# A hybrid recurrent layer: which engine makes the low parts of the input projection's weights

## The chip, the core and the metric

The kernel runs on one core of a Trainium2 chip. The metric is device microseconds of one execution, as the median of the timed runs; lower is better. The engines are named TensorE (PE in the rows; PEld is its weight load), VectorE (DVE), ScalarE (ACT), GpSimd (POOL) and SyncE (SP, whose queue issues nearly all the DMAs). Each engine works through a queue of its own in order, and waits where an instruction needs the result of another engine.

## What is computed

One layer of a hybrid decoder, for 1024 prompt tokens and 64 sample tokens (8 sequences of 8) together. Only the parts that matter here:

```python
z = jnp.einsum('bld,de->ble', x, p['w_in'])          # 1024 -> 2828 columns
(a_x, a_gate, b_xbc, b_dt, b_gate, c_qkv, c_beta, c_decay, c_gate, d_u, d_gate) = split_cols(z, IN_SPLITS)
ya = rglru_mixer(a_x, ...) * silu(a_gate)            # A: RG-LRU
yb = rms_norm(ssd_mixer(b_xbc, b_dt, ...) * silu(b_gate))   # B: Mamba-2 SSD
yc = gdn_mixer(c_qkv, c_beta, c_decay, ...) * silu(c_gate)  # C: gated delta net
yd = s5_mixer(d_u, ...) * silu(d_gate)               # D: S5
x = layer_norm(ALPHA * x + concat(ya, yb, yc, yd) @ p['w_out'])
```

All of it is float32, with float32 results; the new states of the four mixers are returned too.

## The kernel before

**The products.** TensorE multiplies float32 in three passes: each operand is split into a high part (a copy to the type fp32r) and a low part (the operand less the high part), and the product is high times high, low times high and high times low (L226, L227, L228 for the input projection). `xh` and `xl` hold the input, transposed, 8 tiles of 128 rows by 1088 tokens.

**The channel tiles.** The input projection makes most of its columns as channel tiles, called strips here: 128 channels by 1088 tokens, in three blocks of tokens (320, 384, 384), each a PSUM bank. `gemm_ch` does one strip. It calls `load_w` for the strip's weights, then multiplies block after block; `evac` empties each bank to SBUF, on ScalarE (L242) or, every fourth time, on VectorE (L244). There are 18 strips through `gemm_ch`: six of C_QKV (in the order 2, 3, 0, 1, 4, 5), two of C_AX, four of C_XBC, two gates each for A, D and C. The two strips of C_DU have code of their own (`u_tiles`), and the token-major weights (`gemm_tok`, L398 to L400) call `load_w` with four parts of 128x536.

**The weights.** `load_w` brings a strip's 128x1024 weights in two parts of 128x512. Each part is a DMA into `wr` (two buffers, L151), a copy to the high part `wh` on ScalarE (L156), and a subtraction into the low part `wl` (L157). `wh` and `wl` have four buffers each, which is two strips. So a strip's weights can be made while the strip before is multiplied, and the high part waits until TensorE has left the strip before that. A buffer of `wr` can be loaded again when its low part is made. `lo_eng` is a list that holds VectorE and is never given another engine.

**What is around it.** The S5 mixer runs between the first strips, in two halves. In each half `table` makes a table of powers (L463 to L465 through `cmul`; on VectorE for the first half, on GpSimd for the second), `outs` makes the output weights on GpSimd (L618 to L620), and `half_run` multiplies the table with S5 inputs on VectorE (L463 to L465 again) and scans (L650). `cmul` and `outs` share four temporary buffers. After a C_QKV strip `conv_of` does its convolution (L264 on ScalarE, L266 three times on VectorE) and `keep_tail` copies its last columns on GpSimd (L270, L271). GpSimd also writes the strip's pad columns (L249, L250). From about 200 us on, `gdn` (chunk by chunk, with a matrix inverse in six levels, L846 to L868) is merged with `side`, which holds the other strips, the RG-LRU, the SSD and the output projection. `gdn` uses GpSimd for L801, L824, L839, L901 and L999.

**What sets the order.** The kernel is written with a framework that derives all semaphores, and that also orders each engine's queue itself, from its own estimates of when an instruction can start. The order on an engine is therefore not simply that of the text.

Of the kernel before, what the change touches and what calls it, by code (L numbers as in the profile page):

```python
# [8 lines left out]
F32 = mybir.dt.float32  # L9
# [5 lines left out]
OP = mybir.AluOpType  # L15
# [4 lines left out]
P = 128  # L20
# [22 lines left out]
def seqs(ap):  # L43

    return ap.rearrange("p (b e) -> p b e", e=11)


def toks(ap):
    return ap.rearrange("p (b e) -> p b e", e=8)
# [3 lines left out]
def hybrid_step(ctx, tc, I, O, dbg=None):  # L53
# [4 lines left out]
    V = nc.vector  # L58
    G = nc.gpsimd
# [17 lines left out]
    def nm(s):  # L77
        uid[0] += 1
        return f"{s}_{uid[0]}"
# [9 lines left out]
    def strip(pool, dt=F32, name="s"):  # L89
        return pool.tile([P, SW], dt, name=nm(name), tag="s")  # L90
# [21 lines left out]
    def merge(*streams):  # L112

        live = [[g, 0.0, w] for g, w in streams]
        while live:
            e = min(live, key=lambda e: e[1] / e[2])
            try:
                c = next(e[0])
                e[1] += c
                yield c  # L120
            except StopIteration:
                live.remove(e)
# [14 lines left out]
        c0 = 0 if i == 0 else NS + P * (i - 1)  # L137
        nc.sync.dma_start(x[:n, :1024], I["x"][c0:c0 + n])

    lo_eng = [V]  # L140

    def load_w(src, n, kn=4, pool=None, ready=None):

        his, los = [], []
        if pool is not None:
            kp = 8 if 8 * n <= SW else 4
            big = [[strip(pool, F32R, name=nm_)[:, :kp * n].rearrange("p (k n) -> p k n", k=kp) for _ in range(8 // kp)] for nm_ in ("wh", "wl")]
        for k0 in range(0, 8, kn):
            wr = wp.tile([P, 536], F32, name=nm("wr"), tag="wr", bufs=2)
            wv = wr[:, :kn * n].rearrange("p (k n) -> p k n", k=kn)  # L150
            nc.sync.dma_start(wv, src[:, k0:k0 + kn])  # L151
            if pool is None:
                hv_, lv = (wp.tile([P, 536], F32R, name=nm(t), tag=t)[:, :kn * n].rearrange("p (k n) -> p k n", k=kn) for t in ("wh", "wl"))
            else:
                hv_, lv = (z[k0 // kp][:, k0 % kp:k0 % kp + kn] for z in big)
            act(hv_, wv, AF.Copy)  # L156
            lo_eng[0].tensor_tensor(lv, wv, hv_.bitcast(F32), OP.subtract)  # L157
            his += [hv_[:, k] for k in range(kn)]
            los += [lv[:, k] for k in range(kn)]
        return his, los  # L160

    def w_tile(c0):
        return I["w_tiles"][W_TILES.index(c0)]
# [57 lines left out]
    def gemm_block(w, a, b, evac):  # L221
        whi, wlo = w
        ps = gemm_bank()
        o = ps[:, :b - a]
        for k in range(8):
            mm(o, whi[k], xh[:, k, a:b], start=(k == 0), stop=False)  # L226
            mm(o, whi[k], xl[:, k, a:b], start=False, stop=False)  # L227
            mm(o, wlo[k], xh[:, k, a:b], start=False, stop=(k == 7))  # L228
        evac(a, b, o)

    def gemm_ch(c0, evac):
        w = load_w(w_tile(c0), P)
        for a, b in BLOCKS:
            gemm_block(w, a, b, evac)
            yield 3.7
# [10 lines left out]
    def gemm_strip(c0, key, i, pool):  # L246

        s = strip(pool, name="z")
        G.memset(s[:, 0:3], 0.0)  # L249
        G.tensor_copy(seqs(s[:, 1027:SW])[:, :, 0:3], cached(key, i))  # L250

        def evac(a, b, o):
            if a == 0:
                copy_out(seqs(s[:, 1027:SW])[:, :, 3:11], toks(o[:, :NS]))
                copy_out(s[:, 3:3 + b - NS], o[:, NS:])
            else:
                copy_out(s[:, 3 + a - NS:3 + b - NS], o)

        yield from gemm_ch(c0 + P * i, evac)
        return s  # L260
# [20 lines left out]
    def new_tails():  # L281
        return tmp("tails")[:, :162].rearrange("p (t e) -> p t e", e=27)

    def store_tails(gt, nt, key):
        nc.sync.dma_start(O[key], gt[:, :nt])
# [105 lines left out]
    def gemm_tok():  # L391
        whi, wlo = load_w(I["w_tok"], 268, 2, cs)
        for i in range(9):
            c0 = 0 if i == 0 else NS + P * (i - 1)
            ps = pg.tile([P, 512], F32, name=nm("pg"), tag="g")
            o = ps[:, :268]
            for k in range(8):
                mm(o, xh[:, k, c0:c0 + P], whi[k], start=(k == 0), stop=False)  # L398
                mm(o, xl[:, k, c0:c0 + P], whi[k], start=False, stop=False)  # L399
                mm(o, xh[:, k, c0:c0 + P], wlo[k], start=False, stop=(k == 7))  # L400
            z = strip(cs, name="bg")
            t, g = z[:, :268], z[:, 268:524]
            act(t, o, AF.Copy)
            act(g, t[:, 4:260], AF.Tanh, scale=0.5)
            act(raw[:, i, 0:4], t[:, 0:4], AF.Copy)
            act(raw[:, i, 4:12], t[:, 260:268], AF.Copy)
            stt(g, g, 1.0, t[:, 4:260], OP.add, OP.mult)
            nc.sync.dma_start(bg_d[i], g)
# [885 lines left out]
    def conv_of(s, wkey, bkey, i, nt, tails, silu=True):  # L1294
        acc = conv(s, wkey, bkey, i, nt)
        keep_tail(s, tails[:, i])
        if silu:
            silu_compact(s, acc)
        return s if silu else acc

    def conv_in(c0, key, wkey, bkey, i, nt, pool, tails, silu=True):
        s = yield from gemm_strip(c0, key, i, pool)
        return conv_of(s, wkey, bkey, i, nt, tails, silu)
# [23 lines left out]
    def gate(c0, pool):  # L1327

        g = strip(pool, name="gate")

        def evac(a, b, o):
            act(g[:, a:b], o, AF.Tanh, scale=0.5)
            stt(g[:, a:b], g[:, a:b], 1.0, o, OP.add, OP.mult)

        yield from gemm_ch(c0, evac)
        return g

    def side():
        lo_eng[0] = V
        bw_ = tc.tile_pool(name="bw", bufs=1, reuse_waits="tile")  # L1340
        bw = bw_.__enter__()
        tails, xc, zb = new_tails(), [], []
        for i in range(2):
            xc.append((yield from conv_in(C_AX, "cache_rglru_conv", "rg_conv_w", "rg_conv_b", i, 2, up, tails, silu=False)))
        store_tails(tails, 2, "rg_tails")

        def ahead():
            for i in range(4):
                zb.append((yield from gemm_strip(C_XBC, "cache_ssd_conv", i, up)))

        hA = []
        yield from merge((rglru(bw, up, xc, hA), 20.0), (ahead(), 44.0))
        for i in range(2):
            g = yield from gate(C_AG + P * i, up)
            stt(toks(g[:, :NS]), toks(g[:, :NS]), 0.5, seqs(hA[i][:, NP:CL])[:, :, 3:11], OP.mult, OP.mult)
            stt(g[:, NS:T], g[:, NS:T], 0.5, hA[i][:, :NP], OP.mult, OP.mult)
            mix[i] = g
        tails = new_tails()
        for i in range(4):
            conv_of(zb[i], "ssd_conv_w", "ssd_conv_b", i, 4, tails)  # L1360
            yield 0.0
        store_tails(tails, 4, "ssd_tails")
        yield from merge((ssd(bw, up, zb[0:2], zb[2], zb[3]), 40.0), (gates_cd(), 44.0))
        mix[2:4] = zb[0:2]
        bw_.__exit__(None, None, None)
        yield from project()
# [3 lines left out]
    def gates_cd():  # L1370
        for i in range(2):
            g = yield from gate(C_DG + P * i, up)
            y = strip(cc, name="yD")
            nc.sync.dma_start(y[:, :T], zd_d[i])
            gv = g[:, :T].rearrange("p (c t) -> p c t", t=8)
            stt(gv, gv, 0.25, y[:, :T].rearrange("p (t c) -> p c t", t=8), OP.mult, OP.mult)
            mix[6 + i] = g
        for i in range(2):
            gc[i] = yield from gate(C_CG + P * i, cc)


    def project():
# [18 lines left out]
        for i in range(9):  # L1401
# [44 lines left out]
            else:  # L1446
                for e in (slice(0, 512), slice(512, 1024)):
                    stt(y[:, e], y[:, e], mv[:, 0:1], lnp[0][:, e], OP.subtract, OP.mult)
                for e in (slice(0, 512), slice(512, 1024)):
                    stt(y[:, e], y[:, e], rs, lnp[1][:, e], OP.mult, OP.add)  # L1450
                    nc.sync.dma_start(dst[:, e], y[:, e])

    run(merge((gdn(wk, up, q, k, v, *rn), 130.0), (side(), 280.0)))


# [77 lines left out]
```

## Time and profile before

| | |
|---|---|
| median of 3 runs | 652.92 us (647.18 to 653.27) |
| the profiled execution | 648.38 us, span 646.5 us |
| instructions | 11718 |
| ScalarE busy | 271.6 us, 42% of the span |
| mean granted TensorE clock | 0.976 |

The span goes from the first to the last instruction of the profiled execution; 1.9 us of its time lie around it. The rows below are from this execution. Times in them are in microseconds from the start of the span.

### The profile page before, as it was taken

What the parts mean: (1) busy time and instruction counts of PE and PEld (TensorE: products, weight loads), DVE (VectorE), ACT (ScalarE), POOL (GpSimd) and SP (SyncE); (2) the same over time, 40 slices, a digit from 0 to 9 for tenths busy, and PEclk for the clock granted to TensorE, in tenths of its full rate; (3) what the DMA queues carried; (4) which work ended last, traced back from release to release, by engine and by line L of the source; (5) the groups of instructions that cost most, each with busy time, mean ns of one, the idle gap of its engine ahead of it and who ended that gap; (6) DMA issues with size and microseconds to landing.
All of it is one profiled execution on the core that took longest, in us unless ns stands there. A gap on an engine that the chain in (4) does not pass through costs nothing.

```text
span 646.5 us, 11718 instructions
## 1 busy us (share of the span) xinstructions
PE 589.7 (91%) x4284; PEld 504.0 (78%) x4284; DVE 469.6 (73%) x1378; ACT 271.6 (42%) x677; POOL 180.9 (28%) x305
## 2 busy tenths in 40 slices
PE   3999699499999999988999999999999796999995
PEld 3999699499999786777888877778777564778884
DVE  5996963782559676899897777868777897754443
ACT  5544235143345244854644434354443752333210
POOL 8313119400101322331502032032030122443633
PEclk9999799889899999999999999999999997999998
DMA  8462113032311010100122021001022511013131
GB/s 288 165 191 63 41 34 86 1 96 59 128 57 55 18 36 33 33 18 19 33 69 68 33 89 66 1 17 43 9 75 78 171 43 49 33 55 113 66 117 78
DMA packets 23929, 44.11 MB, mean 68 GB/s; under 512 B 3073, under 2 KB 10193, under 8 KB 23873
## 3 DMA queue, kind: packets, MB, share of 16 engines
q1 hardware_dynamic: 23696, 42.71, 20.1%
q8 instruction: 33, 0.54, 0.4%
q0 software_dynamic: 176, 0.67, 0.3%
q14 instruction: 24, 0.19, 0.1%
HBM read 32.97 MB, written 10.41 MB: 67 GB/s over the span
## 4 chain that ended last, share of the span: by engine, by line
PE 66%; DVE 19%; POOL 5%; issue 5%; ACT 2%; DMA 1%; SPq 0%; DVEq 0%; ACTq 0%; POOLq 0%
PE pg L226 8%; PE pg L227 8%; PE pg L228 8%; PE pg L1428 5%; PE pg L1427 5%; PE pg L1426 5%; DVE tb L846 2%; DVE yb L846 2%; DVE acc L266 2%; PE ssq L755 1%; PE pg L398 1%; DMA x<-in_x_t_dram 1%; PE pg L399 1%; PE pg L400 1%; PE kq L817 1%
## 5 line engine op out<-in xcount | busy, mean ns | idle before, releaser
L226 PE MATMUL pg<-xh,wh 128*128 128x384 f32 (+1 forms) x432 | 150.2, 348 | 9.0 <-DVE z L244 9.0
L227 PE MATMUL pg<-xl,wh 128*128 128x384 f32 (+1 forms) x432 | 149.0, 345 | 0.0
L228 PE MATMUL pg<-xh,wl 128*128 128x384 f32 (+1 forms) x432 | 147.0, 340 | 0.0
L226 PEld LDWEIGHTS pg<-xh,wh 128*128 128x128 f32 x432 | 82.8, 192 | 12.5 <-DVE z L244 9.3
L227 PEld LDWEIGHTS pg<-xl,wh 128*128 128x128 f32 x432 | 82.6, 191 | 2.1 <-issue 0.5
L228 PEld LDWEIGHTS pg<-xh,wl 128*128 128x128 f32 x432 | 82.4, 191 | 1.3 <-issue 0.3
L1426 PE MATMUL pg<-woh,wh 128*128 128x512 f32 (+1 forms) x144 | 58.2, 404 | 1.9 <-ACT wh L1415 1.9
L1427 PE MATMUL pg<-wol,wh 128*128 128x512 f32 (+1 forms) x144 | 58.5, 406 | 0.2
L1428 PE MATMUL pg<-woh,wl 128*128 128x512 f32 (+1 forms) x144 | 57.9, 402 | 0.4 <-DVE wl L1416 0.4
L266 DVE SCALAR_TENSOR_TENSOR acc<-z,pcol,acc 128x1112 f32<-128x1112 f32 x36 | 49.6, 1381 | 5.1 <-ACT acc L264 4.8
L864 ACT ACTIVATE XY<-XY 128x256 f16<-128x256 f32 (+1 forms) x51 | 19.4, 381 | 53.8 <-PE XY L862 48.2
L156 ACT ACTIVATE wh<-wr 128x512 fp32r<-128x512 f32 (+1 forms) x40 | 25.2, 633 | 35.0 <-PE pg L227 28.3
L1429 DVE SCALAR_TENSOR_TENSOR y<-y,pg 128x512 f32<-128x512 f32 (+1 forms) x18 | 12.3, 686 | 32.2 <-PE pg L1428 28.4
L1426 PEld LDWEIGHTS pg<-woh,wh 128*128 128x128 f32 (+1 forms) x144 | 26.6, 184 | 8.9 <-ACT wh L1415 2.2
L1428 PEld LDWEIGHTS pg<-woh,wl 128*128 128x128 f32 (+1 forms) x144 | 26.6, 185 | 7.3 <-DVE wl L1416 0.9
L1427 PEld LDWEIGHTS pg<-wol,wh 128*128 128x128 f32 (+1 forms) x144 | 26.5, 184 | 7.2 <-DVE wol L1393 1.0
L157 DVE TENSOR_TENSOR wl<-wr,wh 128x512 fp32r<-128x512 f32 (+1 forms) x40 | 28.2, 704 | 2.8 <-ACT wh L156 2.4
L857 DVE TENSOR_TENSOR T<-T,lev 128x256 f16<-128x256 f32 (+1 forms) x51 | 21.4, 419 | 10.7 <-PE T L855 10.1
L868 ACT ACTIVATE XY<-XY 128x256 f16<-128x256 f32 (+1 forms) x51 | 19.4, 381 | 22.5 <-PE XY L867 22.5
L242 ACT ACTIVATE z<-pg 128x384 f32<-128x384 f32 (+2 forms) x37 | 14.0, 389 | 34.5 <-PE pg L228 33.2
L846 DVE COPY tb<-T 64x256 f16<-64x256 f16 x99 | 26.2, 264 | 1.6
L846 DVE COPY yb<-XY 64x256 f16<-64x256 f16 x99 | 23.8, 240 | 4.4 <-ACT XY L868 3.0
(453 smaller groups left out, 1398.0 us busy)
## 6 DMA issues: line engine op xcount, KB each, us to landing
wr<-in_w_tiles_dram SPq DMA_DIRECT2D x40, 256.0 KB, 2.9
x<-in_x_t_dram SPq DMA_DIRECT2D x8, 544.0 KB, 6.3
wo<-in_w_out_dram SPq DMA_DIRECT2D x16, 256.0 KB, 2.9
y<-in_x_dram SPq DMA_DIRECT2D x8, 512.0 KB, 3.3
out_y_dram<-y SPq DMA_DIRECT2D x7, 512.0 KB, 2.6
bgd<-bg SPq DMA_DIRECT2D x9, 128.0 KB, 1.8
dud<-us SPq DMA_DIRECT2D x2, 544.0 KB, 4.2
U<-dud SPq DMA_DIRECT2D x16, 68.0 KB, 3.4
```

Of the source, the lines that this page charges most:

```text
L156: act(hv_, wv, AF.Copy)
L157: lo_eng[0].tensor_tensor(lv, wv, hv_.bitcast(F32), OP.subtract)
L226: mm(o, whi[k], xh[:, k, a:b], start=(k == 0), stop=False)
L227: mm(o, whi[k], xl[:, k, a:b], start=False, stop=False)
L228: mm(o, wlo[k], xh[:, k, a:b], start=False, stop=(k == 7))
L266: stt(acc[:, :CL], s[:, j:j + CL], col(wkey, j * nt + i), acc[:, :CL], OP.mult, OP.add)
L846: V.tensor_copy(dst[s, :, s], src[s])
L857: tt(t_[:n], pt[:n], lev[:n, l].unsqueeze(1).to_broadcast([n, 4, 64]), OP.mult)
L864: act(XY[:n, :256], px[:n, :256], AF.Copy)
L1426: mm(ps[:n], mh[k_], woh[:, k_, e], start=(k_ == 0), stop=False)
L1427: mm(ps[:n], mh[k_], wol[:, k_, e], start=False, stop=False)
L1428: mm(ps[:n], ml[k_], woh[:, k_, e], start=False, stop=(k_ == 7))
```

## The change

`load_w` gets an argument `eng` in place of one that was not used, and subtracts on that engine, or on VectorE if none is given. `gemm_ch` gives GpSimd. The list `lo_eng` goes.

```diff
@@ -137,9 +137,8 @@
-    lo_eng = [V]
-
-    def load_w(src, n, kn=4, pool=None, ready=None):
+
+    def load_w(src, n, kn=4, pool=None, eng=None):
@@ -154,7 +153,7 @@
             act(hv_, wv, AF.Copy)
-            lo_eng[0].tensor_tensor(lv, wv, hv_.bitcast(F32), OP.subtract)
+            (eng or V).tensor_tensor(lv, wv, hv_.bitcast(F32), OP.subtract)
@@ -229,7 +228,7 @@
     def gemm_ch(c0, evac):
-        w = load_w(w_tile(c0), P)
+        w = load_w(w_tile(c0), P, eng=G)
@@ -1336,7 +1335,6 @@
     def side():
-        lo_eng[0] = V
```

The 36 subtractions of the 18 strips thus go to GpSimd. Those of the token weights and of C_DU stay on VectorE.

## Rows read from the trace of the kernel before

**Rows 1.** The page: engine, busy us (share of the span), instructions.
```profile
PE 589.7 (91%) x4284; PEld 504.0 (78%) x4284; DVE 469.6 (73%) x1378; ACT 271.6 (42%) x677; POOL 180.9 (28%) x305
```
**Rows 2.** Windows: length, busy us of each engine (instructions), clock, DMA.
```profile
95.00:130.00 35.00, 25.80 (x193) 24.57 (x192) 19.97 (x38) 13.83 (x25) 25.07 (x54) 0.91 0.17 48
140.00:500.00 360.00, 349.12 (x2803) 297.05 (x2804) 274.39 (x751) 166.77 (x423) 72.83 (x133) 1.00 0.15 49
200.00:440.00 240.00, 230.84 (x1930) 190.71 (x1928) 193.25 (x512) 114.21 (x287) 56.83 (x98) 1.00 0.12 38
```
**Rows 3.** TensorE's waits: who waited for whom, us, times, longest.
```profile
PE pg L374 <- ACT xh L187: 10.5, 1, 10.5
PE pg L226 <- DVE z L244: 9.0, 1, 9.0
PE XY L862 <- DVE yb L846: 6.6, 5, 5.0
PE pg L398 <- ACT bg L403: 5.8, 1, 5.8
```
**Rows 4.** GpSimd's timeline: start, us, instruction, count, idle before and releaser.
```profile
95.75 0.33 POOL L270 COPY tails<-z 128x3 f32<-128x3 f32 x1 [8.77 <-ACT z L242]
...
112.07 1.06 POOL L618 TENSOR_TENSOR cm<-bk,s5p 128x512 f32<-128x512 f32 x1
...
115.83 1.28 POOL L620 TENSOR_TENSOR lo<-cm,cm 128x512 f32<-128x512 f32 x1
...
118.21 1.62 POOL L620 TENSOR_TENSOR lo<-cm,cm 128x512 f32<-128x512 f32 x1
119.78 0.65 POOL L270 COPY tails<-z 128x3 f32<-128x3 f32 x1
```
**Rows 5.** VectorE's timeline from 116 to 130 us.
```profile
117.15 1.53 DVE L463 TENSOR_TENSOR cm<-tab,G 128x512 f32<-128x512 f32 x1 [10.38 <-POOL lo L620]
118.60 1.78 DVE L464 TENSOR_TENSOR cm<-tab,G 128x512 f32<-128x512 f32 x1
120.31 0.68 DVE L463 TENSOR_TENSOR cm<-tab,G 128x512 f32<-128x512 f32 x1
...
129.25 0.41 DVE L244 COPY z<-pg 128x256 f32<-128x256 f32 x1
```
**Rows 6.** Line 157: count, ns min/median/max, first and last start, forms.
```profile
L157 DVE TENSOR_TENSOR wl<-wr,wh x40: 673/686/1049, 26.1 to 440.2; 128x512 fp32r<-128x512 f32 x36, 128x536 fp32r<-128x536 f32 x4
```
**Rows 7.** Line 156: ScalarE's idle time before it, by releaser, us, times.
```profile
  PE pg L227: 28.3, 21
```
**Rows 8.** Timelines of VectorE and TensorE: low parts made, strips multiplied.
```profile
134.14 0.68 DVE L157 TENSOR_TENSOR wl<-wr,wh 128x512 fp32r<-128x512 f32 x1
...
112.90 0.31 PE L226 MATMUL pg<-xh,wh 128*128 128x320 f32 x1
...
141.56 0.30 PE L228 MATMUL pg<-xh,wl 128*128 128x320 f32 x1
```
**Rows 9.** ScalarE's timeline from 92 to 117 us.
```profile
92.60 0.63 ACT L156 ACTIVATE wh<-wr 128x512 fp32r<-128x512 f32 x1 [1.15 <-PE pg L227]
94.68 0.63 ACT L156 ACTIVATE wh<-wr 128x512 fp32r<-128x512 f32 x1 [1.45 <-PE pg L227]
...
112.92 0.63 ACT L156 ACTIVATE wh<-wr 128x512 fp32r<-128x512 f32 x1 [1.48 <-PE pg L227]
...
116.62 0.23 ACT L242 ACTIVATE z<-pg 128x64 f32<-128x64 f32 x1 [1.33 <-PE pg L228]
```
**Rows 10.** VectorE's groups by line from 200 to 440 us: busy, mean ns, idle.
```profile
L157 DVE TENSOR_TENSOR wl<-wr,wh 128x512 fp32r<-128x512 f32 x19 | 13.7, 718 | 2.1 <-ACT wh L156 1.9
```
**Rows 11.** The chain that ended last, its low parts, first and last of six.
```profile
208.84 0.69 DVE wl L157
...
440.24 0.69 DVE wl L157
```
**Rows 12.** The window after TensorE's longest gap but one, columns as in rows 2.
```profile
129.80:134.00 4.20, 4.20 (x13) 4.20 (x14) 4.20 (x8) 0.00 (x0) 0.00 (x0) 0.50 0.00 0
```

## The prediction, made before the changed kernel ran

> **What bounds the kernel now.** I read the page first, then stretches, then who waited for whom, then the two places where a low part is made early or late.
>
> The page's busy times [rows 1] say that TensorE is the bound, at 91% of the span, that VectorE is second at 73%, and that GpSimd has 72% of its time free. Read by stretch [rows 2], from 140 to 500 us TensorE is idle for 360.00 - 349.12 = 10.9 us in all: nothing done there to another engine can give back more than that. From 95 to 130 us it is different: TensorE is busy 25.80 of 35 us, and GpSimd 25.07.
>
> The waits of TensorE [rows 3] name what the stretch average hides. The largest is the start (10.5 us, loading), the next 9.0 us for one VectorE copy, L244, which empties a PSUM bank. Those below are shorter, most of them gdn's; none is for a low part.
>
> Why that copy was late is read in the chain of work and on two queues. GpSimd [rows 4] waits 8.77 us at L270 and then builds the second S5 half's table and `lo` products without a break, until its first L620 ends at 117.1. VectorE [rows 5] has idled 10.38 us for that and then runs the S5 products; L244 stands in its queue behind most of them, at 129.25. TensorE starts again when it has ended, at 129.7. So between 95 and 130 us GpSimd, not TensorE, sets the pace, and each microsecond put on its queue ahead of L620 is a microsecond of TensorE idle unless the order changes too.
>
> **What is removed.** 36 of the 40 instructions of L157 leave VectorE [rows 6]. At the median 0.686 us that is 36 x 0.686 = 24.7 us of 469.6. The other four (the token weights, 128x536) stay. The wait for the high part goes with them to GpSimd.
>
> **What it costs GpSimd.** No low part of weights runs on GpSimd in this trace. The nearest row is L620 [rows 4]: a subtraction of two full 128x512 f32 tiles, 1.28 us alone and 1.62 us where VectorE is also at work. The output type differs (fp32r), which no GpSimd row shows. I take 1.28, with 1.06 (L618, one operand repeated) and 1.62 as ends. 36 x 1.28 = 46 us: GpSimd goes from 180.9 to about 227 us, 35% of the span. As a sum that fits easily.
>
> **Is a low part needed so early that 0.6 us more matters?** A strip's low parts are made while the strip before it multiplies. The buffers allow that: `wh` and `wl` have four, two strips' worth, and ScalarE's waits before L156 are for TensorE to leave an old buffer (28.3 us in 21 waits [rows 7]). The smallest lead that I found is in [rows 8]: strip 1 of C_QKV has its first low part done at 134.82 and is multiplied with it from 141.56, 6.7 us later; the other strips have more. There VectorE made it late, behind the S5 products; GpSimd has it sooner. A low part that takes 0.6 us longer, or waits for one other GpSimd instruction, is still there in time. Reloading `wr` waits for the low part too, so the weight DMAs on SP's queue, and what stands behind them, shift by the same 0.6 us or so; ScalarE's wait for an old buffer comes after them [rows 7]. What is queued on GpSimd behind a low part that waits for its high part: L270's tails, the pads of the next strip, and from 200 us on gdn's L801, L824, L839 and L999, for which VectorE and so TensorE wait. GpSimd is busy 56.83 of 240 us there [rows 2], 19 low parts more make it 81, and I cost that, lead and DMA at nothing. The cover is the 6.7 us; were it gone, TensorE would stand still for whatever is over.
>
> **Where the change is on the path: 92 to 130 us.** Two strips fall into it. Strip 0's high parts end on ScalarE at 93.2 and 95.3 [rows 9]. GpSimd is idle then, waiting at L270 until 95.75, so the first low part is free. The second starts at 95.3 and ends at 96.6, or it follows L270. Either way the S5 table starts about one low part later: +1.3 us. The ends are 0 (both behind the S5 work, which strip 0, multiplied from 112.90 [rows 8], can't stand for long) and 2 x 1.62 = 3.2. Strip 1's second high part ends at 113.5, in the middle of the S5 work. L270 of the strip before it, ready then too, was put behind L620, to 119.78 [rows 4], so I put strip 1's low parts there, at 120 to 124. They then run beside VectorE's S5 products. How that goes is seen at 117.15: two such products took 1.53 and 1.78 us while GpSimd was still at its S5 products, until 119.8, against 0.68 afterwards [rows 4, 5]. That is +0.85 and +1.10, so two low parts cost VectorE about 2.0 us ahead of L244. The ends are 0 (behind L244) and 3.2. TensorE waits for L244, so both terms go into its 9.0 us gap: +3.3 us.
>
> The Trainium skill (SBUF — State Buffer, section "SBUF: two separate sides") says it as a rule: a GpSimd instruction and a VectorE instruction with two SBUF inputs need one shared port pair, and whichever starts first holds it to its end. The trace agrees: the two stretched products each have two SBUF inputs. By that rule alone all 36 low parts would stop VectorE for their whole length; that is rival 2.
>
> **Where the relief is worth something: 200 to 440 us.** There 19 low parts took 13.7 us of VectorE [rows 10], which is busy 193.25 of 240 us [rows 2]. TensorE idles 240 - 230.84 = 9.2 us. The chain of work that ended last goes through six low parts in all, 0.60 to 0.69 us each [rows 11], 4.0 us. Those are the ones where the next VectorE instruction was waited for. The ends are 0 (TensorE's queue, nearly full, takes the place) and 4.0 us. I take half, 2.0: TensorE's queue is 96% full there, and where a link goes the queue itself takes its place.
>
> **The sum.** 648.4 (the profiled execution, span 646.5 and 1.9 around it) + 1.3 + 2.0 - 2.0 = 649.7 us, said as 650. The three timed runs of before lie on both sides of the profiled one, 647.18 to 653.27, with the median at 652.92. So 1%, about what a measurement of this kernel can tell from no change, is also about what its own runs differ by.
>
> **Rivals.**
>
> 1. *GpSimd becomes the pacer of the S5 half (slower).* All four low parts of strips 0 and 1 stand ahead of L620, each stretched to 1.62 us: 6.5 us later. TensorE's gap grows from 9.0 to 15.5 us. After the gap TensorE runs 4.2 us at a granted clock of 0.50, 1.2 GHz [rows 12]; they cost 2.1, and a longer gap may double that. 648.4 + 6.5 + 2.1 = 657. For it: GpSimd has no hole from 96 to 120. Against it: L270, also ready, was not let in before 119.78. It decides from the third low part ahead of L620 on.
>
> 2. *The port takes back more than is freed (slower).* Each low part stops VectorE for its 1.28 us: in 200 to 440 us 19 x 1.28 = 24.3 in place of 13.7, +10.6 us on an engine busy 81% there. With the 3.3 of the S5 stretch that is 648.4 + 10.6 + 3.3 = 662. For it: rows 5. Against it: it takes VectorE to want the port all the time; many of its instructions in gdn (L822, L823, L857) read PSUM and only one tile of SBUF. Shown at less than full price it merges into the main case.
>
> 3. *VectorE was the hidden pacer (faster).* The freed 13.7 us take most of TensorE's 9.2 us idle of that stretch: 648.4 - 9.2 + 1.3 = 640.5. For it: VectorE stands behind most of the short waits of TensorE. Against it: those waits end on gdn's own serial steps, of which only six on the chain stood behind a low part.
>
> 4. *The queues are reordered and L244 comes first (faster).* The order of each queue is made by the framework from its estimates, not by the program text. L244's bank is full by 116.6, when ScalarE empties its share of it [rows 9]; were it copied before the S5 products, the 9.0 us gap and the 2.1 us at half clock would go: 648.4 - 11.1 = 637.
>
> That TensorE waits for GpSimd at every strip I leave out: 6.7 us is the smallest lead [rows 8], and a low part on GpSimd is under 2 us.
>
> **Chances.** Main case 0.54 (range 645 to 655); rival 1 0.14, rival 2 0.07, other losses by reordering 0.02; rival 3 0.13, rival 4 0.10. So faster by over 1% 0.23, within 1% 0.54, slower by over 1% 0.23. The range of 8 in 10 leaves out rival 4's end and rival 2's: 640 to 660.
>
> **What would show it.** L157 of GpSimd near 1.28 us each, 36 times, and four left on VectorE. VectorE's busy time down by 18 to 25 us (lower than 24.7 by what the port adds). Strip 0's second low part ahead of the S5 table on GpSimd and strip 1's behind L620, S5 products on VectorE of over 1 us beside them, and TensorE's wait for L244 at 10 to 13 us. No TensorE wait named for `wl`. Wrong would be: a TensorE wait for `wl` or L244 over 15 us, GpSimd low parts at 2 us and more, TensorE's idle time from 140 to 500 us down to 4 us or up past 18, or the 9 us gap gone.

## The result, and the profile after

The changed kernel takes 668.40 us (667.72 to 669.39) where the kernel before took 653.10 in the same comparison: a ratio of 1.0278, 95% interval 1.0232 to 1.0324. It is slower by 2.8%, and the forecast was no change. Disturbed executions are left out of every ratio here (one of h_tiny_ordb at 1099 us, whose profile is not used either, and two of b2_v_peorda near 680 us), and a ratio is estimated from all the other runs, so it isn't always the quotient of two medians. The lines of the changed kernel stand one number lower than before (L156 is the low part, L225 to L227 the products, L243 VectorE's bank copy, L845 gdn's small copies).

The page's busy line, as in [rows 1], of an execution with a span of 666.5 us:
```profile
PE 599.5 (90%) x4284; PEld 510.4 (77%) x4284; DVE 475.7 (71%) x1342; ACT 271.5 (41%) x677; POOL 229.7 (34%) x341
```
VectorE lost 36 instructions and is busy 6.1 us *more* (469.6 before). TensorE does the same 4284 instructions in 9.8 us more busy time, and it is idle 666.5 - 599.5 = 67.0 us where it was 646.5 - 589.7 = 56.8. So the 20.0 us of the two spans are 9.8 us of slower matmuls and 10.2 us of idle time.

The low parts by line, as in [rows 6], and GpSimd's idle time ahead of them:
```profile
L156 POOL TENSOR_TENSOR wl<-wr,wh x36: 1266/1285/2479, 35.8 to 458.2; 128x512 fp32r<-128x512 f32 x36
...
  ACT wh L155: 85.2, 23
```
The median of 1.285 us is what the row of L620 promised. GpSimd now stands 85.2 us at low parts whose high part is not made.

The windows, columns as in [rows 2]:
```profile
95.00:130.00 35.00, 25.73 (x193) 24.50 (x192) 20.03 (x31) 14.11 (x25) 29.49 (x57) 0.91 0.21 63
140.00:500.00 360.00, 342.64 (x2686) 290.39 (x2687) 265.01 (x675) 162.38 (x404) 108.13 (x160) 0.98 0.14 46
200.00:440.00 240.00, 223.73 (x1844) 185.72 (x1843) 186.23 (x459) 110.50 (x270) 79.01 (x113) 0.98 0.13 39
```
From 95 to 130 us TensorE's busy time hardly changed, since the longer gap ends just behind that window. From 200 to 440 us TensorE idles 240 - 223.73 = 16.3 us in place of 9.2, and gets 1844 instructions done in place of 1930, VectorE 459 in place of 512. More than half of the time went there and behind it; 8.8 of 19.9 us were lost by 208.9 us (table under "Where in the kernel").

TensorE's waits, as in [rows 3]:
```profile
PE pg L225 <- DVE z L243: 11.8, 1, 11.8
PE pg L373 <- ACT xh L186: 10.8, 1, 10.8
PE XY L861 <- DVE T L856: 7.0, 7, 2.4
```
In the kernel before the last of these was:
```profile
PE XY L862 <- DVE T L857: 3.1, 4, 1.4
```
No wait is for a strip's `wl`. The gap behind the bank copy grew from 9.0 to 11.8 us; that behind gdn's T grew from 3.1 to 7.0.

The S5 stretch on GpSimd and on VectorE, as in [rows 4] and [rows 5]:
```profile
93.58 1.31 POOL L156 TENSOR_TENSOR wl<-wr,wh 128x512 fp32r<-128x512 f32 x1 [6.38 <-ACT wh L155]
95.66 1.28 POOL L156 TENSOR_TENSOR wl<-wr,wh 128x512 fp32r<-128x512 f32 x1 [0.77 <-ACT wh L155]
96.87 0.19 POOL L269 COPY tails<-z 128x3 f32<-128x3 f32 x1
...
119.20 1.62 POOL L619 TENSOR_TENSOR lo<-cm,cm 128x512 f32<-128x512 f32 x1
120.78 3.38 POOL L156 TENSOR_TENSOR wl<-wr,wh 128x512 fp32r<-128x512 f32 x2
```
```profile
121.29 1.75 DVE L462 TENSOR_TENSOR cm<-tab,G 128x512 f32<-128x512 f32 x1
122.97 1.75 DVE L464 TENSOR_TENSOR gd<-cm,cm 128x512 f32<-128x512 f32 x1
124.63 0.68 DVE L463 TENSOR_TENSOR cm<-tab,G 128x512 f32<-128x512 f32 x1
...
132.38 0.41 DVE L243 COPY z<-pg 128x256 f32<-128x256 f32 x1
```
Strip 0's second low part stands ahead of the S5 table, strip 1's two stand behind the last `lo` product, two VectorE products beside them take 1.75 us, and the bank copy comes at 132.38 in place of 129.25.

### The profile page after: what moved, and what is told of

The parts are those of the page before. It is cut to its first block, busy times and chain, and to the rows that moved or that the text cites. A ratio compares the mean times of both kernels' runs of the same rounds, so it can differ in the third digit from the quotient of the medians.

```text
span 666.5 us, 11703 instructions
## 1 busy us (share of the span) xinstructions
PE 599.5 (90%) x4284; PEld 510.4 (77%) x4284; DVE 475.7 (71%) x1342; ACT 271.5 (41%) x677; POOL 229.7 (34%) x341
## 4 chain that ended last, share of the span: by engine, by line
PE 68%; DVE 19%; POOL 6%; ACT 3%; issue 3%; DMA 1%; SPq 0%; DVEq 0%; ACTq 0%; POOLq 0%
PE pg L225 9%; PE pg L226 8%; PE pg L227 8%; PE pg L1426 5%; PE pg L1424 4%; PE pg L1425 4%; DVE acc L265 2%; DVE yb L845 2%; DVE tb L845 2%; PE ssq L754 1%; DMA x<-in_x_t_dram 1%; PE kq L816 1%; PE pg L397 1%; PE yd L1092 1%; DVE cm L462 1%
## 5 line engine op out<-in xcount | busy, mean ns | idle before, releaser
L225 PE MATMUL pg<-xh,wh 128*128 128x384 f32 (+1 forms) x432 | 153.4, 355 | 11.8 <-DVE z L243 11.8
L227 PE MATMUL pg<-xh,wl 128*128 128x384 f32 (+1 forms) x432 | 149.6, 346 | 0.0
L225 PEld LDWEIGHTS pg<-xh,wh 128*128 128x128 f32 x432 | 84.2, 195 | 15.4 <-DVE z L243 12.1
L226 PEld LDWEIGHTS pg<-xl,wh 128*128 128x128 f32 x432 | 84.6, 196 | 2.5 <-issue 1.2
L227 PEld LDWEIGHTS pg<-xh,wl 128*128 128x128 f32 x432 | 84.4, 195 | 1.5 <-issue 0.2
L156 POOL TENSOR_TENSOR wl<-wr,wh 128x512 fp32r<-128x512 f32 x36 | 49.6, 1380 | 85.4 <-ACT wh L155 85.2
L265 DVE SCALAR_TENSOR_TENSOR acc<-z,pcol,acc 128x1112 f32<-128x1112 f32 x36 | 51.5, 1430 | 4.9 <-ACT acc L263 4.6
L1427 DVE SCALAR_TENSOR_TENSOR y<-y,pg 128x512 f32<-128x512 f32 (+1 forms) x18 | 12.3, 686 | 32.7 <-PE pg L1426 32.6
L845 DVE COPY yb<-XY 64x256 f16<-64x256 f16 x99 | 28.9, 292 | 6.0 <-ACT XY L867 4.7
L845 DVE COPY tb<-T 64x256 f16<-64x256 f16 x99 | 28.7, 290 | 2.6 <-PE XY L866 1.0
```

What stands on the lines that cost most here:

```text
L156: (eng or V).tensor_tensor(lv, wv, hv_.bitcast(F32), OP.subtract)
L265: stt(acc[:, :CL], s[:, j:j + CL], col(wkey, j * nt + i), acc[:, :CL], OP.mult, OP.add)
L845: V.tensor_copy(dst[s, :, s], src[s])
```

## The experiments

The framework's own order of the queues differs between the two kernels. TensorE's matmuls part at 188.7 us of the kernel before (193.5 of the changed one); VectorE's and ScalarE's queues differ earlier. To take it out, a run's queues were tied to the order read from one of the two kernels, with one ordering edge (no semaphore) from each instruction to the next on its engine (shortened):

```python
for n in order[engine]:
    tc.add_manual_dep(here[n], last, order_only)   # instruction n stands behind the one before it
    last = here[n].name
```

"Order of before" means this for all five engines; low parts on GpSimd fall in where the framework puts them. A run's time is given with its ratio to the kernel before in the same comparison, and that ratio's 95% interval. Idle is TensorE's span less its busy time, in the profiled execution.

| run | us, median | ratio | TensorE busy / idle | VectorE busy |
|---|---|---|---|---|
| before | | 1 | 589.7 / 56.8 | 469.6 |
| changed kernel | 668.40 | 1.0278 [1.0232, 1.0324] | 599.5 / 67.0 | 475.7 |
| a_g_ordb | 662.84 | 1.0178 [1.0134, 1.0222] | 594.3 / 64.9 | 477.5 |
| b_v_orda | 659.84 | 1.0134 [1.0068, 1.0200] | 601.9 / 57.8 | 470.9 |
| c_none_ordb | 648.62 | 0.9968 [0.9943, 0.9993] | 591.3 / 54.4 | 449.6 |
| f_dummy_ordb | 662.81 | 1.0170 [1.0118, 1.0222] | 595.6 / 66.5 | 487.8 |
| h_tiny_ordb | 648.93 | 0.9974 [0.9942, 1.0005] | | |
| g_pieces_ordb | 660.70 | 1.0158 [1.0118, 1.0198] | 597.4 / 62.4 | 467.5 |
| e_late_ordb | 658.78 | 1.0127 [1.0081, 1.0173] | 595.3 / 62.8 | 472.0 |
| b2_v_peorda | 672.63 (665.40 of the two counted) | 1.0230 [1.0170, 1.0290] | 597.0 / 66.8 | 471.6 |
| n_g_peordb | 679.72 | 1.0444 [1.0369, 1.0519] | 607.1 / 69.5 | 477.6 |
| k_v_l244 | 648.99 | 0.9986 [0.9952, 1.0020] | 596.3 / 50.5 | 469.7 |
| l_g_l244 | 661.42 | 1.0162 [1.0112, 1.0212] | 600.3 / 60.7 | 477.4 |
| after_again | 665.54, one run | | 597.0 / 66.8 | 475.3 |

h_tiny_ordb, which does the work of the kernel before with its queues tied, is no slower than it: tying the queues costs nothing by itself.

### GpSimd or VectorE, the one order or the other

a_g_ordb is the changed `load_w` in the order of before; b_v_orda is `load_w` on VectorE in the order of the changed kernel.

> GpSimd makes the 36 low parts, and every queue is kept in the order that it had in the kernel before (the low parts fall in where the framework puts them on GpSimd). Theory order (the 15 us come from the queues that the framework arranged anew): with the old order the time comes back to that of before, 648 to 656 us. Theory port (a low part on GpSimd stops VectorE for about 1 us each, 24 us over the kernel, so the relief is eaten): the order changes little, 660 to 668 us, and VectorE's busy time stays at about 475 us. Theory queue (GpSimd, in order, stands at low parts whose high part is not made, and gdn's small GpSimd steps behind it are late): 660 to 668 us too, with the wait for L156 ahead of GpSimd's L157 at 80 us and more, and TensorE's gaps behind gdn's GpSimd steps.

> VectorE makes the 36 low parts as before, and every queue is kept in the order that it has in the changed kernel. Theory order: the time is that of the changed kernel, 662 to 670 us, though no low part is on GpSimd. Theory port and theory queue: both causes are gone, so 648 to 656 us.

Each half alone is slower: GpSimd by 1.8% in the old order, the new order by 1.3% with nothing on GpSimd. The two add up to 3.1%, where both together measured 2.8%; the intervals allow the same. They cost in different ways: a_g_ordb has 8.1 us more idle time of TensorE and 4.6 us more busy time than before, b_v_orda 1.0 and 12.2. The busy time goes with the clock: the mean granted clock is 0.976 before, 0.966 in a_g_ordb and 0.961 in b_v_orda. So no theory stands alone. "Order" is wrong about a_g_ordb, "port" and "queue" about b_v_orda.

### What the relief is worth, and what GpSimd takes for it

> No engine makes the 36 low parts (the third product takes the high part in their place, so this computes something else, for the time alone); queues in the order of before. It gives the upper bound of what relieving VectorE can bring, 24.7 us of its work gone with nothing put elsewhere. My prediction's step, relief -2.0 with ends 0 and -4.0 and the S5 terms gone, says 645 to 650 us. If VectorE were the hidden pacer (rival 3 of the prediction): 638 to 642 us. Theory port takes the difference between this run and the one with GpSimd in the same order as the price of the low parts on GpSimd: 12 to 20 us.

```diff
-            (eng or V).tensor_tensor(lv, wv, hv_.bitcast(F32), OP.subtract)
+            eng is None and V.tensor_tensor(lv, wv, hv_.bitcast(F32), OP.subtract)
-            los += [lv[:, k] for k in range(kn)]
+            los += [(lv if eng is None else hv_)[:, k] for k in range(kn)]
```
With the low parts gone altogether the kernel gains 0.3%, 2 us (at most 0.6% by the interval, 3.7 us). Even that may not be the relief: h_tiny_ordb, with the same order and no relief at all, has 0.9974, and the profiled spans are 645.7 and 646.5 us. So the whole relief is worth between nothing and 3.7 us. c_none_ordb and a_g_ordb have the same VectorE instructions in the same order, and VectorE is busy 449.6 us in the one and 477.5 in the other. So the 36 low parts on GpSimd cost VectorE 27.9 us, 0.78 each. Made by VectorE itself they cost it 469.6 - 449.6 = 20.0.

How it loses them is seen in the same stretch of gdn in both. VectorE in c_none_ordb, as [rows 5]:
```profile
258.72 1.32 DVE L1212 SCALAR_TENSOR_TENSOR r<-aq,r 128x1112 f32<-128x1112 f32 x1
259.95 0.45 DVE L846 COPY yb<-XY 64x256 f16<-64x256 f16 x2
260.42 0.85 DVE L888 TENSOR_TENSOR Yf<-XY,F 64x256 f32<-64x256 f16 x2
261.28 0.41 DVE L892 TENSOR_TENSOR x<-XY,F 64x256 f32<-64x256 f16 x1
```
VectorE in a_g_ordb:
```profile
213.17 0.47 DVE L822 SCALAR_TENSOR_TENSOR A<-kq,beta,gam 64x64 f32<-64x64 f32 x2
213.56 0.27 DVE L823 TENSOR_TENSOR Pm<-kq,gam 64x128 f32<-64x128 f32 x1
...
263.83 1.32 DVE L1212 SCALAR_TENSOR_TENSOR r<-aq,r 128x1112 f32<-128x1112 f32 x1
265.07 2.53 DVE L846 COPY yb<-XY 64x256 f16<-64x256 f16 x2
267.61 0.85 DVE L888 TENSOR_TENSOR Yf<-XY,F 64x256 f32<-64x256 f16 x2
268.48 0.41 DVE L892 TENSOR_TENSOR x<-XY,F 64x256 f32<-64x256 f16 x1
```
GpSimd in a_g_ordb:
```profile
213.15 1.29 POOL L157 TENSOR_TENSOR wl<-wr,wh 128x512 fp32r<-128x512 f32 x1 [0.64 <-PE kq L817]
...
264.43 3.09 POOL L157 TENSOR_TENSOR wl<-wr,wh 128x512 fp32r<-128x512 f32 x2 [0.65 <-PE F L886]
```
TensorE in a_g_ordb:
```profile
269.04 0.83 PE L896 MATMUL J<-x,A 64*64 64x64 f32 x8 [2.06 <-DVE x L892]
```
Two copies of 64x256 f16 take 0.45 us in the one and 2.53 in the other. They end at 267.6, with GpSimd's two low parts (264.43 to 267.5). TensorE then waits 2.06 us for L892, three instructions further on. At 213 us, on the other hand, L822 and L823, which read PSUM, run through at 0.27 us and less each while a low part is under way from 213.15 to 214.44, as fast as in c_none_ordb.

### The price without the work, and the wait without the price

f_dummy_ordb leaves the low parts on VectorE and adds to each a subtraction on GpSimd that nobody reads; h_tiny_ordb does the same with 8 columns in place of 416 (shortened):

```diff
+            eng is None or XTRA.append(G.tensor_tensor(dm[:], hv_[:, :416], hv_[:, :416], OP.subtract))
```

> VectorE makes the 36 low parts as before, in the order of before; beside them GpSimd does 36 subtractions of 128x416 on the same high parts into a buffer that nobody reads, so nobody needs their result. Theory port: 36 x about 1 us x 0.8 of stretch on VectorE with no relief at all: VectorE busy 485 to 495 us, the time 10 to 20 us over before, 660 to 675 us. Theory queue: the dummies wait for the high part like the low parts do, so the time also rises, 656 to 668 us, but VectorE's busy time stays at 470 to 475 us. Theory order: 648 to 656 us.

> VectorE makes all low parts, order of before; GpSimd does 36 subtractions of only 128x8 on the same high parts into a buffer that nobody reads. They wait for the high part in GpSimd's queue like the low parts did in the run with GpSimd in the order of before, but hold nothing for long. Theory queue (what costs is that GpSimd's queue stands still at the wait): most of the +11 us stays, 658 to 664 us. Theory port (what costs is the 1.28 us in which VectorE is stopped): gone, 648 to 654 us, VectorE busy 468 to 474 us.

The dummy costs 1.7%, as much as the real low parts, though no instruction needs its result and VectorE was relieved of nothing; VectorE's busy time rises by 487.8 - 469.6 = 18.2 us. The tiny one, which stands at the same wait in GpSimd's queue, costs nothing. So it is the time for which GpSimd works that costs, and not the place in its queue. That time could also make GpSimd's own results late. In the gdn stretch it doesn't: from 205 to 515 us VectorE waits for GpSimd for 8.2 us in the kernel before, 6.7 in a_g_ordb and 7.2 in f_dummy_ordb, and TensorE never does. "Queue" falls.

### Shorter pieces

The edit, shortened; it holds for the strips alone:

```diff
-            (eng or V).tensor_tensor(lv, wv, hv_.bitcast(F32), OP.subtract)
+            for j in range(kn): G.tensor_tensor(lv[:, j], wv[:, j], hv_[:, j].bitcast(F32), OP.subtract)
```

> Each of the 36 low parts is made on GpSimd in four instructions of 128x128 in place of one of 128x512, order of before. Theory port, held to the end of each instruction: a VectorE instruction is then stopped for at most about 0.35 us at a time and can start between two pieces; the +11 us fall to +3 to +7 us, 654 to 658 us, and the longest stretch of a VectorE copy L846 falls from 2 us to under 1.5. If VectorE lost the whole hold in any case: 661 to 665 us as with one piece. Theory queue: no change, 661 to 665 us.

The time missed the expected 654 to 658 us. But the loss has moved. From the first block of the eighth strip (208.9 us before) to the last matmul of the strips, TensorE loses 11.3 - 8.6 = 2.7 us against before, and 12.0 - 4.2 = 7.8 with whole low parts. Ahead of that strip it loses 8.6 in place of 4.2. Four pieces hold GpSimd longer than one instruction (144 of 0.462 us at the median, 80.7 us busy in all), and that is a loss of its own ahead of gdn: 3.1 us at the third strip's last block (2.1 with whole low parts), and more between the fifth and seventh strips, where TensorE waits 2.2 us for S5's gate (L706, L707) and its half-clock stretch is 3.4 us longer. Beside a low part a copy L846 now takes at most 0.50 us, where it took up to 1.30. VectorE's cost falls to 467.5 - 449.6 = 17.9 us. Shorter holds help where VectorE can slip in between; the run as a whole can't show that alone.

### Where in the kernel

> GpSimd makes the low parts of the last 12 strips only (24 of 36); the six of C_QKV stay on VectorE; order of before. In the run with all 36 on GpSimd TensorE came to the third block of the third strip 2.7 us later than with no low parts at all, which is the S5 stretch of the prediction (1.3 + 2.0), and had lost 4.5 us by the seventh strip and 13.7 at the end of the strips. If the two places are independent, this run has the second loss only: TensorE's gap ahead of L226 behind L244 is 9.0 us again, and the time is 656 to 660 us. If the loss in the gdn stretch came from what was late before it: 650 to 654 us.

The list `n` is kept from call to call (shortened):

```diff
-        w = load_w(w_tile(c0), P, eng=G)
+        w = load_w(w_tile(c0), P, eng=G if n.append(0) or len(n) > 6 else None)
```
How late TensorE is against the kernel before, from its timelines (us; the third strip is strip 0 of C_QKV):

| first matmul of | before, at | c_none_ordb | e_late_ordb | a_g_ordb | b_v_orda | changed |
|---|---|---|---|---|---|---|
| third strip, block 3 | 129.7 | -0.6 | +0.7 | +2.1 | -0.7 | +3.1 |
| seventh strip | 194.5 | -0.3 | +2.5 | +4.2 | +4.1 | +4.9 |
| eighth strip | 208.9 | -0.4 | +3.3 | +4.2 | +7.3 | +8.8 |
| end of the strips | 504.5 | -1.8 | +10.7 | +12.0 | +13.6 | +19.9 |

With the first six strips on VectorE the S5 gap is 9.0 us again, the ratio is 0.5% below that of a_g_ordb (the intervals overlap), and the loss of the gdn stretch is all there: from the seventh strip on 10.7 - 2.5 = 8.2 us, and 9.7 against c_none_ordb, which gains 1.5 there. So the gdn loss doesn't need the S5 loss ahead of it, as expected. That e_late_ordb is 2.5 us late already at the seventh strip was not expected; 1.7 of it is a half-clock stretch at 182.9, shown further down. The S5 stretch costs 2.7 us (a_g_ordb less c_none_ordb), from there to the seventh strip 1.8 more (1.7 of it one half-clock stretch at 194.3), and from the seventh strip on the low parts cost (12.0 + 1.8) - (4.2 + 0.3) = 9.3. The windows from there to the end of the strips, in c_none_ordb and in a_g_ordb:
```profile
194.20:502.70 308.50, 298.50 (x2489) 246.43 (x2488) 236.22 (x682) 145.53 (x385) 68.43 (x117) 1.00 0.13 43
```
```profile
198.70:516.40 317.70, 300.22 (x2490) 247.87 (x2489) 249.63 (x682) 146.08 (x386) 98.46 (x138) 0.99 0.13 43
```
TensorE is idle 10.0 us in the one and 17.5 in the other, and 1.7 us more is busy time, which is half of one 3.40 us stretch at half clock at 269.4. VectorE does the same 682 instructions in 13.4 us more.

### What in the order costs

> VectorE makes the low parts as before; only TensorE's queue is kept in the order of the changed kernel, the other queues are the framework's own. If the +8 us of the changed kernel's order lie in TensorE's own order (which matmuls are mixed with which, and so where its clock falls to 0.50): 657 to 664 us, with half-clock stretches near 185, 205, 291 and 305 us. If they lie in the other queues: 648 to 655 us, without them.

> The changed kernel with TensorE's queue alone kept in the order of before; the other queues are the framework's own. The changed kernel was 5.6 us slower than GpSimd in the full order of before. If those lie in TensorE's own order: 660 to 665 us. If in the other queues: 666 to 671 us. Below 658 us the reading that the port alone takes some 11 us falls.

> The changed kernel once more, one profile. If its half-clock stretches of TensorE belong to its order of queues, they stand at the same places as in its first profile (near 185, 206, 295, 308 us besides those that the kernel before has too) and TensorE's busy time is 597 to 602 us again; if they come and go with the execution, they stand elsewhere, and busy time and span change with them.

Neither mixed order is better than an order that is whole: TensorE in the new order with the other queues arranged around it has 1.0230, not clear of b_v_orda's 1.0134; TensorE in the old order in the changed kernel has 1.0444, the slowest of all. Both times lie above every range expected of them (665.40 and 679.72). The half-clock stretches expected of b2_v_peorda near 185, 205, 291 and 305 us are not there (it has others, at 220 and 421). In both runs the framework arranged the other queues anew, so they don't tell in which queue the 1.3% lie. What can be said is how they cost. The windows of three stretches, in the kernel before, as [rows 2]:
```profile
185.40:188.80 3.40, 3.40 (x21) 3.40 (x20) 1.23 (x1) 2.11 (x3) 0.00 (x0) 1.00 0.02 5
205.80:209.20 3.40, 3.40 (x32) 2.76 (x31) 2.65 (x5) 1.61 (x5) 1.15 (x2) 1.00 0.12 43
308.20:311.60 3.40, 3.40 (x29) 3.06 (x29) 3.40 (x4) 3.32 (x7) 2.99 (x2) 1.00 0.25 77
```
In the changed kernel, and one more at 294.6:
```profile
185.40:188.80 3.40, 3.40 (x14) 3.40 (x14) 2.70 (x2) 0.00 (x0) 0.15 (x1) 0.50 0.25 77
205.80:209.20 3.40, 3.37 (x11) 2.98 (x12) 3.40 (x8) 0.91 (x4) 0.00 (x0) 0.51 0.00 0
294.60:298.00 3.40, 3.40 (x22) 2.78 (x21) 2.41 (x5) 1.90 (x4) 0.31 (x1) 0.50 0.01 2
308.20:311.60 3.40, 3.40 (x21) 2.79 (x18) 2.30 (x6) 0.70 (x2) 0.00 (x0) 0.51 0.03 3
```
In its second execution:
```profile
185.40:188.80 3.40, 3.40 (x15) 3.40 (x15) 2.32 (x2) 0.00 (x0) 1.18 (x1) 0.51 0.24 75
205.90:209.30 3.40, 3.40 (x12) 3.07 (x13) 3.40 (x7) 0.91 (x4) 0.00 (x0) 0.50 0.00 0
294.60:298.00 3.40, 3.40 (x29) 2.75 (x27) 3.29 (x6) 3.15 (x6) 1.34 (x1) 1.00 0.01 2
308.30:311.70 3.40, 3.40 (x19) 2.79 (x17) 2.69 (x13) 0.38 (x1) 0.00 (x0) 0.50 0.00 0
```
And in b_v_orda, where VectorE makes the low parts:
```profile
184.80:188.20 3.40, 3.40 (x14) 3.40 (x14) 1.39 (x2) 0.00 (x0) 0.00 (x0) 0.51 0.22 77
205.30:208.70 3.40, 3.40 (x13) 3.40 (x12) 3.37 (x9) 0.45 (x4) 0.00 (x0) 0.50 0.00 0
290.60:294.00 3.40, 3.40 (x16) 3.09 (x15) 3.04 (x8) 1.59 (x3) 0.00 (x0) 0.51 0.00 0
304.30:307.70 3.40, 3.40 (x18) 2.77 (x17) 3.00 (x11) 0.64 (x2) 0.00 (x0) 0.50 0.29 80
```
Three of the four return at the same places in a second execution, and all four in b_v_orda; the one near 295 comes and goes. Each costs half of its 3.40 us, so that four cost 6.8 of the 12.2 us of busy time that b_v_orda loses. Those at 206, 295 and 308 stand behind TensorE waits of 1.2 to 2.4 us (for VectorE's b or z, tb and T) that the kernel before does not have or has shorter. What of the new order makes these waits was not settled.

The one at 185 stands behind no wait, but behind eighteen matmuls of two columns each (L755 of the kernel before), which TensorE does in the same place of its queue in both orders. In the changed kernel:
```profile
183.28 2.17 PE L754 MATMUL ssq<-half,sq 128*128 128x2 f32 x18
```
In the kernel before the same eighteen run from 179.97 to 182.14; the windows right behind them, in the kernel before and in e_late_ordb (180.86 to 183.03), whose queues have the order of before:
```profile
182.20:185.60 3.40, 3.40 (x23) 3.40 (x23) 1.98 (x4) 1.29 (x3) 0.20 (x1) 1.00 0.26 84
```
```profile
182.90:186.30 3.40, 3.40 (x15) 3.40 (x15) 2.03 (x1) 0.00 (x0) 0.86 (x1) 0.50 0.23 77
```
So the clock can fall there in the order of before too, and this stretch does not belong to the new order alone; why it falls in some runs and not in others is open.

### Is the S5 gap worth closing

> The kernel before with one instruction of VectorE's queue moved: the copy L244 that ended at 129.7 us stands ahead of the second S5 half's products, where VectorE waits for GpSimd anyway. Prediction's reading (TensorE's 9.0 us wait and the half clock after it come from that copy alone): the wait goes, and TensorE then meets the next thing that is late, strip 1's low parts, which VectorE makes behind the S5 products at about 134 (7 us of lead before, so some 4 us of wait if the strip comes 11 us earlier): 4 to 9 us faster, 640 to 646 us. If the gap only moves (S5 late, or the same time lost later): 647 to 653 us.

> The same move with the 36 low parts on GpSimd, order of before else. The run with GpSimd and the order of before was 11 us over the kernel before: some 3 of them ahead of L244, the rest in the gdn stretch. If the two losses are independent, the 3 and the gap go and the rest stays: 650 to 656 us, 7 to 12 us over the run with VectorE and the same move. If GpSimd's low parts gain from being early here (strip 1's are ready before VectorE could make them): up to 4 us less, 646 to 650 us.

In k_v_l244 the bank copy L244 stands ahead of the S5 products, and the 9.0 us wait is gone (idle 50.5 in place of 56.8). The time is the same. TensorE's stretch at half clock, before and in k_v_l244:
```profile
123.80:134.00 10.20, 4.28 (x13) 4.28 (x14) 10.20 (x26) 0.00 (x0) 0.00 (x0) 0.50 0.00 0
```
```profile
127.40:141.00 13.60, 12.45 (x57) 10.43 (x58) 13.15 (x24) 6.19 (x11) 1.17 (x3) 0.50 0.15 44
```
Before, TensorE is mostly idle while its clock is at 0.50 and loses 4.28 / 2 = 2.1 us; now it has work there and loses 12.45 / 2 = 6.2. The next stretch at half clock is 6.8 us long (168.4 to 175.2) in place of 3.4 (171.5 to 174.9), 1.7 us more. TensorE also waits 3.3 us for the S5 state (L676, behind VectorE's L465), where it came too early. TensorE starts that block 9.3 us sooner and the strip after next 1.2 us sooner. The expected wait of 4 us for strip 1's low parts did not come (TensorE waits for no strip's `wl` in that run); the S5 state was late next. l_g_l244 is to a_g_ordb as k_v_l244 is to before: no difference. Its 661.42 us missed the expected 650 to 656: the S5 loss did not go with the gap, and TensorE waits 6.2 us for the S5 state there.

## Why the prediction was wrong

**Costs on GpSimd, right.** 36 at 1.285 us (1.28 foreseen), 229.7 us busy (227), no TensorE wait for `wl`. That GpSimd's queue behind a low part that waits costs nothing was right too: h_tiny_ordb puts the wait there and loses nothing.

**The S5 stretch, right.** One low part ahead of the table, two behind the last `lo` product, two stretched VectorE products, and a gap of 11.8 us where 12.3 was foreseen. The runs put the stretch at 2.7 us (a_g_ordb less c_none_ordb). Rival 1 did not come about, since strip 1's low parts stayed behind L619.

**The relief, inside its ends.** -2.0 with ends 0 and -4.0; c_none_ordb shows between nothing and 3.7 us, so that the half taken as the middle is not shown. Rival 3 falls with it: with its work gone VectorE is still not the pacer.

**The price of GpSimd's low parts in the gdn stretch, wrong: set at nothing, measured at 9.3 us.** The prediction saw in [rows 5] that a VectorE instruction beside a GpSimd one is stopped, charged that in the S5 stretch, and left it out of the sum for 200 to 440 us. Rival 2 carried it, priced at +10.6 there and 662 us in all; a_g_ordb took 662.84. That the numbers agree so well is in part luck: rival 2 lets every low part stop VectorE for its whole 1.28 us, where it was 0.78 on average, and 1.7 us of a_g_ordb's time is the half-clock stretch at 194.3. The step that failed is the argument against that rival, and with it the chance of 0.07: that many of gdn's instructions (L822, L823, L857) read PSUM and only one tile of SBUF. Those are indeed not stopped: L823 takes 0.27 us beside a low part and without one. But the 64x256 copies L846 are, and they have one input and one output in SBUF. So are steps with one tile and a scalar such as L1131 (0.352 us at the median, 1.343 beside a low part) and ones with two tiles such as L266 (1.37 us, up to 2.29 beside a low part). The prediction took a hold on the port to matter for two-input instructions only, since the two rows that it had were of that kind. The trace of the kernel before had the other kind too, on VectorE and on GpSimd in the gdn stretch:
```profile
281.62 2.19 DVE L846 COPY tb<-T 64x256 f16<-64x256 f16 x2
```
```profile
281.65 2.08 POOL L1211 TENSOR_TENSOR aq<-acc 128x1112 f32<-128x1112 f32 x1
```
Two copies, 0.22 us each at the median, take 2.19 us beside GpSimd's 2.08. And gdn's inverse is a serial chain with L846 in every level, so that a stop there reaches TensorE. From the seventh strip to the end of the strips its waits for `yb` of L846 are 1.5 us in c_none_ordb and 4.2 in a_g_ordb, those for T 1.2 and 3.6, those for L892 0.9 and 2.1.

The Trainium skill (SBUF — State Buffer, section "SBUF: two separate sides") names a VectorE instruction in a 2-port mode beside one with two SBUF inputs as the other kind that needs the pair; only the second half of the sentence was used in the prediction. The trace agrees in that one-input copies stop, 0.45 us becoming 2.53 for two; in which mode they ran it does not record.

**The relief was itself returned.** VectorE's busy time was to fall by 18 to 25 us; it rose by 6.1. What a low part takes from VectorE by being beside it (0.78 us) is more than what VectorE saves. TensorE's idle time from 140 to 500 us, 360.00 - 342.64 = 17.4 us, stayed just under the 18 that the prediction named as a sign of being wrong, so that this bound was too wide.

**The order, wrong: set at nothing but a chance of 0.02.** The framework arranged all queues anew (TensorE's matmuls from 188.7 us on), and the new arrangement is worth +1.3% by itself, nearly all of it as TensorE busy time at a lower mean clock (12.2 us busy, 1.0 idle). What in the order does it stays open. The prediction knew that the order is made by the framework, and used that only for a gain (rival 4). That gain isn't there either: moving L244 first closes the gap and the time stays.

## What to carry to other kernels

Before moving an SBUF-to-SBUF operation from VectorE to GpSimd, price it on VectorE twice: what it frees, and what the same number of GpSimd durations takes from whatever VectorE runs beside them, small one-input copies too; on a serial chain much of the second reaches TensorE (here 9.3 us, in a stretch where VectorE took 13.4 us more). An upper bound for the gain is cheap to get by leaving the work out: here it was at most 3.7 us, and in this order of the queues no other place for this work could have won more. And where a framework orders the queues, an edit of one engine changes them all; tie the order of before to tell the edit from the new order.

## What was not expected of the hardware

Small VectorE copies (64x256 f16, SBUF to SBUF, 0.22 us each) stop for a GpSimd instruction until it ends, up to 2.53 us for two, while instructions that read PSUM run through beside one at 0.27 us.

TensorE's clock falls to 0.50 at places that return with the program, and not only behind idle time: at 185.4 us TensorE had no wait ahead of it in either execution of the changed kernel, but eighteen matmuls of two columns, 2.17 us. Behind the same eighteen the kernel before stays at 1.00. And a wait that is removed can leave its half-clock stretch behind, with more work in it: 4.28 us of busy time at 1.2 GHz before, 12.45 with the wait gone.
